# A decoder layer on one core: the prompt's value products one step later, and values stored by block

## The chip, the cores and the metric

The kernel runs on one NeuronCore of a Trainium2 chip. A core has five engines, each with its own queue of instructions that it works through in order: TensorE (PE in the profile; its weight loads are listed apart as PEld), VectorE (DVE), ScalarE (ACT), GpSimd (POOL) and SyncE (SP), which here issues nearly all DMAs. They meet through semaphores. Data are computed on in SBUF (128 partitions); TensorE writes its results to PSUM, eight banks of 2 KB a partition.

The metric is the device time of one execution in microseconds. The kernel before took 1530.84 us in the median of three executions (1525.71 to 1532.65).

## The reference

One layer of a hybrid decoder, for a prompt of 1024 positions and for 8 samples of 8 new positions each, all in fp32. What matters here is the prompt's attention: 16 heads of 64, four query heads to a key/value head, a window of 128 positions, and one learned sink per head that joins the softmax without a value.

```python
def attn_prompt(q, k, v, sinks):
    ...
    kk = jnp.concatenate([jnp.pad(kb, pad)[:, :-1], kb], axis=2)
    vv = jnp.concatenate([jnp.pad(vb, pad)[:, :-1], vb], axis=2)
    diff = jnp.arange(BLOCK)[:, None] + BLOCK - jnp.arange(2 * BLOCK)[None, :]
    band = (diff >= 0) & (diff < WINDOW)
    ...
    o = sink_attention(qb, kk, vv, mask[:, None, None], sinks)

def layer(...):
    h = rmsnorm(x, norm_mix)
    q, k, v, gu, gv, ga, gb = split_in(h @ w_in)
    ...
    s = spatial_gating(jax.nn.gelu(gu), vn, ws, bs)
    merged = jax.nn.sigmoid(ga) * (o @ w_pa) + jax.nn.sigmoid(gb) * (s @ w_pb)
    x = x + merged @ w_out
    f, nconv = conv_ffn(rmsnorm(x, norm_ffn), w_up, conv_w, conv_b, w_down, conv_prev)
    return x + f, nk, nv, nconv, vn
```

A block of 128 queries sees its own block of keys up to the diagonal and the block before it beyond the diagonal. Together these are exactly 128 keys for every query, so one 128 x 128 tile of probabilities holds both: position j of it is the key of the own block where j is at most the query's place, and the key of the block before otherwise.

## The kernel before, in words

Nearly every fp32 number is held as a high and a low part (`split`, lines 39 to 41: ACT casts to the high part, DVE subtracts to get the low one), and a product is made of three matmuls. The 1088 positions go in two groups: the samples with prompt blocks 0 to 3 (group 0), and blocks 4 to 7 (group 1). The program runs through the input projection (to about 440 us), the samples' attention and the attention of group 0 with the gMLP branch's projection between its parts, the attention of group 1 with group 0's merge between its parts (to about 690 us), the output projection and the feed-forward part (to the end).

**Values.** In the projection `v_out` gets 128 positions by 256 values (four key/value heads of 64) for each block, splits them, and stores the tile `ws` of 128 x 4 x 128 (high and low part of each head, 2 KB a partition) in `vd` (line 552). It does the same with differences against the block before (`dvd`). In the attention `values(kv)` loads what a key/value head needs: `vst` with 4 or 5 blocks of values in one DMA (line 950), `dvst` with 3 or 4 blocks of differences in four DMAs of 64 partitions (line 953). Both have two places.

**The loop over steps.** `attention` runs through 16 steps a group, four key/value heads (kv) by four blocks (i). A step has three parts.

- `sc_p` makes the scores (tile `sc`, line 1205, 8 matmuls; 2 KB x 2 of PSUM, one place), copies them to `s` (ACT, line 1213), replaces keys beyond the diagonal by those of the block before (DVE, predicated copy, line 1215; a first block is masked by POOL, line 1218), takes the maximum with the sink (`nm`, line 1221), exponentiates four heads (ACT, line 1224), and scales by the reciprocal of the sums (`dn`, lines 1226 and 1227). `s` has three places.
- `tr_p` transposes the probabilities (`pt`, line 1234, 4 matmuls, one PSUM bank), splits them into `ph` and `pl`, and makes a selection `c` of both on POOL (line 1245, four instructions): the probabilities that belong to the block before.
- `pv_p` makes the value products (`po`, one PSUM bank): four matmuls of `ph` and `pl` with the values (line 1262), then two of `c` with the differences (line 1265), which correct the places of the block before. First blocks have two matmuls (line 1257). ACT copies half of the result (`ot`, line 1268), DVE adds the halves (`of`, line 1273), and a split gives `oh` and `ol`, the attention's output.

Between these parts `fill` puts pieces of other work: in group 0 the branch's projection, in group 1 the merge (matmuls `mm` of line 235, a product `stg` on DVE, loads and stores on SP, weights cast to `wh` and `wl`). A counter deals them out evenly over a number of slots (`slots["of"]`).

The code's order is not quite the order on the engines. The tile layer puts instructions into the queues by its own priorities and costs, so a product may stand a few matmuls ahead of or behind its place in the code. Two places of a tile (`bufs=2`) let a new one be written while the old one is read.

Of the kernel before, what the change touches and what calls it, by code (L numbers as in the profile page):

```python
# [6 lines left out]
F32 = mybir.dt.float32  # L7
F32R = mybir.dt.float32r
# [7 lines left out]
P = 128  # L16
# [6 lines left out]
NKV = 4  # L23
# [11 lines left out]
def layer(tc, a):  # L35
    nc = tc.nc
# [10 lines left out]
    with ExitStack() as top:  # L47
# [280 lines left out]
        dr = lambda name, shape, dt=F32: dram.tile(shape, dt, name=name)  # L328
# [3 lines left out]
        kd = [dr(f"kd{c}", [P, 2, T]) for c in range(2)]  # L332
        gud = [dr(f"gud{c}", [P, T]) for c in range(NG)]
        sgd = [[dr(f"sg{e}d{c}", [P, T]) for c in range(KD)] for e in range(2)]
        vd = dr("vd", [P, NKV, 8, P])
        v3d = dr("v3d", [P, 256])
        dvd = dr("dvd", [P, NKV, 8, P])
        gvd = {name: dr(f"gvd{name}", [P, GW]) for gr in groups for name, _ in gr["toks"]}
        vnd = [dr(f"vnd{gr['g']}", [P, NG, len(gr["toks"]), P]) for gr in groups]
        sd_ = [[dr(f"sd{g}{c}", [P, 2, n]) for c in range(NG)] for g, n in ((0, 576), (1, 512))]  # L340
# [11 lines left out]
        with ExitStack() as ph1:  # L352
# [175 lines left out]
            def v_out(g, i, ps):  # L528
                name = groups[g]["toks"][i][0]
                v = gvp.tile([P, 256], F32, name="gv")  # L530
                S.activation(v, ps, AF.Copy, scale=1.0 if g else rstg[g][:, i:i + 1])
                if name == "s":
                    nc.sync.dma_start(vsd, v[0:NS])
                    for b in range(8):
                        nc.sync.dma_start(a["vsn"][b], v[8 * b:8 * b + 8])
                else:
                    if name == 4:
                        late["v"] = gvp.tile([P, 256], F32, name="gv")
                        nc.sync.dma_start(late["v"], v3d)
                    for to, x in ((vd, v), (dvd, None)):  # L540
                        if x is None and name == 0:
                            continue
                        t = W.sm.tile([P, 4, P], F32, name="ws", bufs=2)
                        tr, four = t.bitcast(F32R), lambda y: y.rearrange("p (h d) -> p h d", d=64)
                        if x is None:
                            x = t[:, :, 64:128]
                            for r, (y, z) in ((0, (v, late["v"])), (64, (late["v"], v))):
                                V.tensor_sub(x[r:r + 64], four(y)[r:r + 64], four(z)[r:r + 64])
                        else:
                            x = four(x)  # L550
                        split(tr[:, :, 0:64], tr[:, :, 64:128], x)
                        nc.sync.dma_start(to[:, :, name], t)
                    late["v"] = v
                    if name == 3:
                        nc.sync.dma_start(v3d, v)
                if name == 7:
                    nc.sync.dma_start(a["vp"], v)
# [362 lines left out]
            def prepare(gr):  # L920

                g, n = gr["g"], gr["n"]
# [3 lines left out]
                at, nk = ((NS, 512), (448, 640))[g]  # L926
# [16 lines left out]
                def values(kv):  # L943

                    def go():
                        if kv < NKV:
                            v = kvp.tile([P, nv, P], F32R, name="vst", bufs=2)
                            d = kvp.tile([P, 2, nd, P], F32R, name="dvst", bufs=2)
                            gr["vst"][kv], gr["dvst"][kv] = v, d
                            nc.sync.dma_start(v.bitcast(F32), vd[:, kv, b0:b0 + nv])  # L950
                            for e in (0, 64):
                                for o in (0, 64):
                                    nc.sync.dma_start(d[o:o + 64, e // 64].bitcast(F32),
                                                      dvd[e:e + 64, kv, b0 + 1:b0 + 1 + nd])
                    return go

                gr["operands"], gr["values"], gr["b0"] = operands, values, b0
# [124 lines left out]
            def attention(gr, pieces):  # L1082
# [3 lines left out]
                if has_s:  # L1086
                    qs, kn, vs, sp = (smp[x] for x in ("qs", "kn", "vs", "p"))
                nblk = 4
                slots = {"n": len(pieces), "done": 0, "at": 0, "of": 40 + (8 if has_s else 0)}

                def fill():
                    slots["at"] += 1
# [96 lines left out]
                with tc.tile_pool(name=f"at{g}", bufs=1) as ap:  # L1189
# [3 lines left out]
                    def sc_p(kv, i):  # L1193
# [12 lines left out]
                                          start=e == 0, stop=e == 1)  # L1206
                        if i == 0:
                            gr["operands"](kv + 1)()
                        if i == 2:
                            gr["values"](kv + 1)()  # L1210
                        s = ap.tile([P, 4, P + 1], F32, name="s", bufs=3)
                        G.tensor_copy(s[:, :, P], late["sinkb"][:, 4 * kv:4 * kv + 4])
# [17 lines left out]
                    def tr_p(kv, i):  # L1230
                        s = st.pop((kv, i))
                        pt = pst.tile([P, 512], F32, name="pt")
                        for h in range(4):
                            PE.transpose(pt[:, h * P:h * P + P], s[:, h, 0:P], ident)
                        ph = ap.tile([P, 512], F32R, name="ph")
                        pl = ap.tile([P, 512], F32R, name="pl")
                        split(ph, pl, pt)
                        parts = []
                        if gr["blk0"] + i:
                            c = ap.tile([P, 512], F32R, name="c")  # L1240
                            cs, fs, ls = (x.rearrange("p (h e q) -> p h e q", h=4, e=2) for x in (c, ph, pl))
                            for src, swap in ((fs, 0), (ls, 1)):
                                for e in range(2):
# [30 lines left out]
                        c0 = soff + P * i  # L1274
                        split(oh[kv][:, :, c0:c0 + P], ol[kv][:, :, c0:c0 + P], of)

                    for i in range(len(steps) + 2):
                        if i >= 2:
                            tr_p(*steps[i - 2])
                        fill()  # L1280
                        if i < len(steps):
                            sc_p(*steps[i])
                        fill()
                        if i >= 2:
                            pv_p(*steps[i - 2])
                if g == 0:
                    mo[1].close()
                    sso.close()
# [650 lines left out]
```

## Time and profile before

| what | us |
|---|---|
| median of three executions | 1530.84 |
| profiled execution, its own time | 1529.31 |
| its span, first to last instruction | 1527.6 |
| samples' attention ahead of the first prompt scores | 465.0 to 494.4 |
| prompt loop of group 0 | 494.4 to 588.0 |
| fillers between the loops | 588.0 to 599.0 |
| prompt loop of group 1 to its last scores | 599.0 to 669.4 |
| its tail, to the last value products | 669.4 to 687.0 |

The profile lists an engine as busy while an instruction of it runs. Matmuls overlap each other (one starts about 0.12 us behind the one before and is listed for about 0.28 us), so PE can look busy in a stretch where it started nothing. Weight loads do not overlap each other like that: where matmuls follow each other without a wait, a weight load is under way all of the time, and idle time of PEld is time lost. A row of waits names the waiting engine, tile and line, then what ended the wait, then the sum in us, how often, and the longest.

### The profile page before, as it was taken

To read this page: it belongs to the slowest core of one execution; us is meant where nothing else is said; L and a number is where in the kernel's file an instruction comes from. 1 tells how busy PE (TensorE), PEld (TensorE's weight loads), DVE (VectorE), ACT (ScalarE), POOL (GpSimd) and SP (SyncE) were. 2 spreads that over 40 slices of the span, in tenths; PEclk is the share of its full clock that TensorE was granted. 3 is DMA by queue.
4 is the path that set the end of the run, shared out by engine and by line. 5 is a ranking of instruction groups with operands and counts; after the bars stand their busy time and mean duration, and the time that the engine had idled before them with its cause. 6 is when DMAs were issued, how large, how long until landed. Compare 5 with 4: busy or idle time off the path is not lost.

```text
span 1527.6 us, 31403 instructions
## 1 busy us (share of the span) xinstructions
PE 1507.0 (99%) x12202; PEld 1489.1 (97%) x12202; DVE 1156.2 (76%) x1918; ACT 823.2 (54%) x1745; POOL 274.9 (18%) x429
## 2 busy tenths in 40 slices
PE   9999999999999999999999999999999999999998
PEld 9999999999998999989999999999999999999997
DVE  6886778756544886889658888898899888785685
ACT  6555764454543674774433555555555556453562
POOL 0000002200120232440122212232232222000002
PEclk9999999999999999999999999999999999999998
DMA  8553447747649857658988432332243226973453
GB/s 285 156 170 126 166 168 257 247 140 270 222 152 327 258 187 217 202 181 301 327 275 275 146 120 92 120 137 100 87 151 107 79 93 214 363 258 96 127 177 130
DMA packets 136357, 286.64 MB, mean 188 GB/s; under 512 B 15248, under 2 KB 43344, under 8 KB 136208
## 3 DMA queue, kind: packets, MB, share of 16 engines
q1 hardware_dynamic: 132176, 281.08, 55.2%
q10 hardware_dynamic: 4032, 3.55, 0.7%
q8 instruction: 96, 1.57, 0.4%
q14 instruction: 53, 0.43, 0.1%
HBM read 195.69 MB, written 90.85 MB: 188 GB/s over the span
## 4 chain that ended last, share of the span: by engine, by line
PE 68%; DVE 5%; ACT 4%; issue 3%; POOL 2%; DMA 2%; SPq 0%; POOLq 0%; ACTq 0%; DVEq 0%
PE st L294 40%; PE dn L1700 13%; PE mm L235 12%; ACT s L1224 2%; POOL c L1245 1%; POOL x L1765 1%; PE sc L1205 1%; PE mx L832 1%; DVE pl L41 1%; DVE nm L1221 1%; DVE s L1227 0%; ACT ot L1268 0%; DVE wl L41 0%; DVE of L1273 0%; DMA wraw<-wpb 0%
## 5 line engine op out<-in xcount | busy, mean ns | idle before, releaser
L294 PE MATMUL st<-th,wh 128*128 128x256 f32 (+1 forms) x2128 | 611.3, 287 | 4.2 <-ACT k L275 2.3
L294 PE MATMUL st<-tl,wh 128*128 128x256 f32 (+1 forms) x2128 | 609.4, 286 | 0.0
L294 PE MATMUL st<-th,wl 128*128 128x256 f32 (+1 forms) x2128 | 608.8, 286 | 0.0
L294 PEld LDWEIGHTS st<-th,wh 128*128 128x128 f32 x2128 | 400.7, 188 | 6.0 <-ACT k L275 3.4
L294 PEld LDWEIGHTS st<-th,wl 128*128 128x128 f32 x2128 | 401.0, 188 | 0.0
L294 PEld LDWEIGHTS st<-tl,wh 128*128 128x128 f32 x2128 | 400.5, 188 | 0.0
L40 ACT CAST wh<-wraw 128x512 fp32r<-128x512 f32 (+2 forms) x204 | 139.6, 694 | 107.0 <-PE st L294 35.4
L41 DVE TENSOR_TENSOR wl<-wraw,wh 128x512 fp32r<-128x512 f32 (+2 forms) x204 | 159.4, 794 | 37.7 <-ACT wh L40 35.5
L1700 PE MATMUL dn<-th,wh 128*128 128x288 f32 (+1 forms) x616 | 176.7, 287 | 0.0
L1700 PE MATMUL dn<-tl,wh 128*128 128x288 f32 (+1 forms) x616 | 176.2, 286 | 0.0
L1700 PE MATMUL dn<-th,wl 128*128 128x288 f32 (+1 forms) x616 | 175.1, 284 | 0.0
L40 ACT CAST wh<-ws 128x512 fp32r<-128x512 f32 x160 | 98.1, 622 | 96.8 <-PE st L294 62.0
L41 DVE TENSOR_TENSOR wl<-ws,wh 128x512 fp32r<-128x512 f32 x160 | 109.5, 697 | 48.5 <-ACT wh L40 46.8
L1700 PEld LDWEIGHTS dn<-th,wl 128*128 128x128 f32 x616 | 115.9, 188 | 0.0
L1700 PEld LDWEIGHTS dn<-tl,wh 128*128 128x128 f32 x616 | 115.7, 188 | 0.0
L1700 PEld LDWEIGHTS dn<-th,wh 128*128 128x128 f32 x616 | 115.6, 188 | 0.0
L282 POOL TENSOR_TENSOR z<-kn,k 128x256 f32<-128x256 f32 (+1 forms) x32 | 29.9, 938 | 320.0 <-ACT kn L277 304.4
L40 ACT CAST th<-traw 128x544 fp32r<-128x544 f32 (+1 forms) x85 | 53.8, 642 | 45.1 <-PE dn L1700 32.6
L41 DVE TENSOR_TENSOR tl<-traw,th 128x544 fp32r<-128x544 f32 (+1 forms) x85 | 61.6, 732 | 21.0 <-ACT th L40 20.6
L235 PE MATMUL mm<-s,wh 128*128 128x256 f32 (+1 forms) x384 | 75.4, 292 | 0.9 <-DMA s<-sd 0.9
L525 PE MATMUL st<-w2h,th 128*128 128x256 f32 x308 | 74.4, 283 | 0.4 <-ACT w2h L40 0.4
L235 PE MATMUL mm<-oh,wh 128*128 128x256 f32 (+1 forms) x256 | 74.0, 289 | 0.0
(292 smaller groups left out, 3178.2 us busy)
## 6 DMA issues: line engine op xcount, KB each, us to landing
wraw<-wt SPq DMA_DIRECT2D x133, 512.0 KB
traw<-td SPq DMA_DIRECT2D x77, 272.0 KB
td<-za SPq DMA_DIRECT2D x22, 544.0 KB
wraw<-wt SPq DMA_DIRECT2D x35, 256.0 KB
upd<-hl SPq DMA_DIRECT2D x14, 512.0 KB
td<-t SPq DMA_DIRECT2D x11, 544.0 KB
qd<-q SPq DMA_DIRECT2D x8, 576.0 KB
q<-qd SPq DMA_DIRECT2D x8, 576.0 KB
```

The lines of the kernel that those rows point to most:

```text
L40: S.copy(hi, src)
L41: V.tensor_sub(lo, src, hi.bitcast(F32))
L235: PE.matmul(ps[:, lo:lo + c1 - c0], u[:, k, :], v[:, c0:c1], start=(k == 0 and i == 0), stop=(k == nk - 1 and i == 2))
L282: op(to, pick(x, to, lo, hi), pick(y, to, lo, hi))
L294: PE.matmul(ps, u[:, kk, :], v, start=first and kk + i == 0, stop=kk == 3 and i == 2, skip_group_check=True)
L525: PE.matmul(ps, u, v[:, k, :], start=k + i == 0, stop=k == KD - 1 and i == 2)
L832: PE.matmul(ps[:, P * i:P * i + P], vn[:, i], late["wst"][:, c, :], start=True, stop=True)
L1205: PE.matmul(ps[:, h, o0:256], q, kst[kv][:, e, k0:cur + P], start=e == 0, stop=e == 1)
L1221: V.tensor_reduce(nm, s, AX.X, ALU.max, negate=True)
L1224: S.activation(s[:, h], s[:, h], AF.Exp, bias=nm[:, h:h + 1], accum_out=dn[:, h:h + 1])
L1245: G.affine_select(cs[w:w + 64, :, e], src[r:r + 64, :, e].bitcast(F32), [[0, 4], [1 - 2 * e, 64]], ALU.is_ge, 0.0, base=-e, channel_multip ...
L1700: PE.matmul(place(m, e), u[:, m, :], v[:, lo:hi], start=new and i + k == 0 and (e == 0 or m % 2 == 0), stop=i == NU - 1 and k == 2, skip_g ...
```

## The change

- The loop makes the value products of a step one iteration later (`pv_p(*steps[i - 3])`), and so has one iteration more at its end, with one filler slot instead of two. The slots are counted as 41 instead of 40 (49 instead of 48 with the samples).
- `ph`, `pl` and `c` get two places each, 6 KB more a partition.
- The values of the next key/value head are loaded in step 3 instead of step 2.
- `vd` and `dvd` lie by block: a block's tile is stored as 128 rows of 2 KB, where each row was four pieces of 512 B, and the loads gather pieces of 512 B, where a partition's row was one piece of 1.5 to 2.5 KB.

```diff
-        vd = dr("vd", [P, NKV, 8, P])
+        vd = dr("vd", [8, P, NKV, P])
...
-        dvd = dr("dvd", [P, NKV, 8, P])
+        dvd = dr("dvd", [8, P, NKV, P])
...
-                        nc.sync.dma_start(to[:, :, name], t)
+                        nc.sync.dma_start(to[name], t)
...
-                            nc.sync.dma_start(v.bitcast(F32), vd[:, kv, b0:b0 + nv])
+                            nc.sync.dma_start(v.bitcast(F32), vd[b0:b0 + nv, :, kv].rearrange("b p d -> p b d"))
...
-                                                      dvd[e:e + 64, kv, b0 + 1:b0 + 1 + nd])
+                                                      dvd[b0 + 1:b0 + 1 + nd, e:e + 64, kv].rearrange(
+                                                          "b p d -> p b d"))
...
-                slots = {"n": len(pieces), "done": 0, "at": 0, "of": 40 + (8 if has_s else 0)}
+                slots = {"n": len(pieces), "done": 0, "at": 0, "of": 41 + (8 if has_s else 0)}
...
-                        if i == 2:
+                        if i == 3:
                             gr["values"](kv + 1)()
...
-                        ph = ap.tile([P, 512], F32R, name="ph")
-                        pl = ap.tile([P, 512], F32R, name="pl")
+                        ph = ap.tile([P, 512], F32R, name="ph", bufs=2)
+                        pl = ap.tile([P, 512], F32R, name="pl", bufs=2)
...
-                            c = ap.tile([P, 512], F32R, name="c")
+                            c = ap.tile([P, 512], F32R, name="c", bufs=2)
...
-                    for i in range(len(steps) + 2):
-                        if i >= 2:
+                    for i in range(len(steps) + 3):
+                        if 2 <= i < len(steps) + 2:
                             tr_p(*steps[i - 2])
                         fill()
                         if i < len(steps):
                             sc_p(*steps[i])
-                        fill()
-                        if i >= 2:
-                            pv_p(*steps[i - 2])
+                        if i < len(steps) + 2:
+                            fill()
+                        if i >= 3:
+                            pv_p(*steps[i - 3])
```

In the rows below the names are the program's tiles as above, a number at a row's start counts the engine's rows, and line numbers of the changed kernel are one higher. First TensorE in the loop of group 1, from a step's transposes to the next value products, before:

```order
4429 L1234 MATMUL pt<-c_ident,s 128x128 x3
4430 L235 MATMUL mm<-oh_6430,wh 128x320
4431 L235 MATMUL mm<-ol_6431,wh 128x320
4432 L235 MATMUL mm<-oh_6430,wl 128x320
4433 L235 MATMUL mm<-oh_6495,wh 128x320
4434 L235 MATMUL mm<-ol_6496,wh 128x320
4435 L1205 MATMUL sc<-kst,q 128x256 x8
4436 L235 MATMUL mm<-oh_6495,wl 128x320
4437 L235 MATMUL mm<-oh_6495,wh 128x320
4438 L235 MATMUL mm<-ol_6496,wh 128x320
4439 L1262 MATMUL po<-ph,vst 128x4x64
```

Here the products read the `ph` made of the transposes at the top. The same stretch in the changed kernel:

```order
4401 L1235 MATMUL pt<-c_ident,s 128x128 x4
4402 L235 MATMUL mm<-ol_6431,wh 128x320
4403 L235 MATMUL mm<-oh_6430,wl 128x320
4404 L235 MATMUL mm<-oh_6430,wh 128x320
4405 L1206 MATMUL sc<-kst,q 128x256 x8
4406 L235 MATMUL mm<-ol_6431,wh 128x320
4407 L235 MATMUL mm<-oh_6430,wl 128x320
4408 L235 MATMUL mm<-oh_6484,wh 128x320
4409 L1263 MATMUL po<-ph,vst 128x4x64
4410 L1263 MATMUL po<-pl,vst 128x4x64
```

The row looks alike, but the products now read the `ph` and `pl` of the transposes one step further up, and all six follow each other where fillers stood between the first two. On VectorE, the last steps of the same loop, before:

```order
745 L1215 COPY_PREDICATED s<-c_mprev,sc 128x4x128
746 L1227 TENSOR_TENSOR s<-s,dn 128x4x128
747 L1273 TENSOR_TENSOR of<-po,ot 64x256 x2
748 L41 TENSOR_TENSOR pl<-pt,ph 128x512
749 L1221 TENSOR_REDUCE nm<-s 128x4
750 L41 TENSOR_TENSOR ol_8564<-of,oh_8563 128x2x128
```

And in the changed kernel:

```order
733 L1216 COPY_PREDICATED s<-c_mprev,sc 128x4x128
734 L1274 TENSOR_TENSOR of<-po,ot 64x256
735 L1222 TENSOR_REDUCE nm<-s 128x4
736 L1274 TENSOR_TENSOR of<-po,ot 64x256
737 L41 TENSOR_TENSOR pl<-pt,ph 128x512
738 L1227 RECIPROCAL dn<-dn 128x4
739 L1228 TENSOR_TENSOR s<-s,dn 128x4x128
740 L41 TENSOR_TENSOR ol_8550<-of,oh_8549 128x2x128
```

A step's maximum moved up to its predicated copy, with only half of an `of` between, and its scaling follows its own maximum instead of the next step's predicated copy.

## The prediction

> **What bounds the kernel now.** I read the page first, then busy time by stage, then the waits of the weight loads in the two prompt loops, then the chain each step of a loop has to pass.
>
> ```profile
> span 1527.6 us, 31403 instructions
> PE 1507.0 (99%) x12202; PEld 1489.1 (97%) x12202; DVE 1156.2 (76%) x1918; ACT 823.2 (54%) x1745; POOL 274.9 (18%) x429
> PE 68%; DVE 5%; ACT 4%; issue 3%; POOL 2%; DMA 2%; SPq 0%; POOLq 0%; ACTq 0%; DVEq 0%
> ```
>
> TensorE is the bound almost everywhere, so only time in which it stands can be won. Busy PE hides that: the chain gives PE 68%, the busy row 99%. Weight loads (PEld) show it better. By stage (columns: PE, PEld, DVE, ACT and POOL busy, clock, DMA share, GB/s):
>
> ```profile
> 512.00:530.00 18.00, 17.91 (x146) 17.57 (x146) 16.03 (x32) 14.31 (x46) 5.86 (x13) 1.00 0.71 225
> 617.00:634.00 17.00, 17.00 (x133) 16.34 (x132) 16.40 (x32) 14.48 (x48) 6.43 (x16) 1.00 0.60 192
> 494.40:588.00 93.60, 91.35 (x717) 86.19 (x716) 76.90 (x147) 63.48 (x200) 28.62 (x71) 1.00 0.63 207
> 588.00:599.00 11.00, 11.00 (x85) 11.00 (x85) 4.35 (x6) 2.01 (x3) 1.25 (x2) 1.00 0.87 273
> 599.00:669.40 70.40, 69.21 (x512) 64.98 (x512) 61.62 (x115) 53.51 (x169) 26.68 (x63) 1.00 0.70 218
> 669.40:687.00 17.60, 16.22 (x120) 14.82 (x119) 13.36 (x26) 10.57 (x30) 8.18 (x15) 1.00 0.51 155
> ```
>
> Between the loops (588 to 599) PEld is busy all of the time, 0.129 us a matmul. In the first loop (494.4 to 588) it is busy 92.1%, in the second (599 to 669.4) 92.3%, in the second's tail, behind its last scores, 84%. The first two rows are the best stretches of each loop: 97.6% and 96.1%. What the weight loads wait for in the first loop, the second, and the second's tail alone:
>
> ```profile
> PEld po L1265 <- POOL c L1245: 2.4, 9, 0.4
> PEld po L1262 <- DVE pl L41: 1.3, 3, 0.5
> ...
> PEld po L1262 <- issue: 0.5, 2, 0.4
> ```
> ```profile
> PEld po L1265 <- POOL c L1245: 5.2, 16, 1.1
> PEld po L1262 <- ACT ph L40: 0.8, 2, 0.5
> ...
> PEld po L1262 <- issue: 0.6, 2, 0.3
> ```
> ```profile
> PEld po L1265 <- POOL c L1245: 2.5, 6, 1.1
> PEld po L1262 <- issue: 0.3, 1, 0.3
> ```
>
> So the value products (po) wait 4.2 us in the first loop and 6.6 in the second, 2.8 of these in the tail. A wait costs more than its idle time:
>
> ```profile
> L1262 PE MATMUL po<-ph,vst x56: 277/283/387, 511.1 to 684.8; 128*128 128x256 f32 x56
> L1265 PE MATMUL po<-c,dvst x56: 277/384/392, 511.6 to 685.7; 128*128 128x256 f32 x56
> ```
>
> The correction products (L1265) take 384 ns in the median, 277 at best. At least 28 of 56 take the longer form: 28 x 0.107 = 3.0 us (an estimate), which I put at 1.2 in the first loop, 1.2 in the second, 0.6 in its tail.
>
> **Products a step later.** Transposes, cast, subtraction and four POOL selects now have a whole step before their products, and ph, pl, c get second places. No instruction is added. All of these po waits can go: 4.2 + 1.2 = 5.4 us in the first loop, 3.8 + 1.2 = 5.0 in the second, 2.8 + 0.6 = 3.4 in its tail, 13.8 in all. What is late next? Prices on PE (chain view of the first loop), DVE and ACT (groups of 600 to 690: busy, mean | idle before):
>
> ```profile
> 507.57 0.44 PE pt L1234 x4
> ...
> 509.03 0.95 PE sc L1205 x8
> ...
> 511.30 0.47 PE po L1262 x4
> ```
> ```profile
> L1273 DVE TENSOR_TENSOR of<-po,ot 64x256 f32<-64x256 f32 x32 | 13.3, 416 | 6.3 <-ACT ot L1268 6.1
> L1227 DVE TENSOR_TENSOR s<-s,dn 128x512 f32<-128x512 f32 x16 | 12.0, 749 | 0.1
> L1215 DVE COPY_PREDICATED s<-c_mprev,sc 128x512 f32<-128x512 int32 x16 | 11.8, 738 | 0.5 <-ACT s L1213 0.4
> L41 DVE TENSOR_TENSOR pl<-pt,ph 128x512 fp32r<-128x512 f32 x16 | 11.0, 689 | 0.4
> L1221 DVE TENSOR_REDUCE nm<-s 128x4 f32<-128x516 f32 x16 | 10.9, 681 | 0.2
> L41 DVE TENSOR_TENSOR wl<-wraw,wh 128x1024 fp32r<-128x1024 f32 x7 | 8.8, 1255 | 0.0
> L41 DVE TENSOR_TENSOR ol<-of,oh 128x256 fp32r<-128x256 f32 x16 | 7.3, 457 | 0.7 <-ACT oh L40 0.5
> L1075 DVE TENSOR_TENSOR stg<-stg,mm 128x576 f32<-128x576 f32 x7 | 5.2, 746 | 5.4 <-PE mm L235 5.4
> L1226 DVE RECIPROCAL dn<-dn 128x4 f32<-128x4 f32 x16 | 2.8, 172 | 2.8 <-ACT s L1224 2.8
> ```
> ```profile
> L1224 ACT ACTIVATE s<-s,nm 128x129 f32<-128x129 f32 x64 | 25.0, 395 | 2.8 <-DVE nm L1221 2.7
> ...
> L40 ACT CAST ph<-pt 128x512 fp32r<-128x512 f32 x16 | 9.4, 587 | 0.3
> ...
> L1213 ACT COPY s<-sc 128x512 f32<-128x512 f32 x16 | 9.3, 582 | 9.2 <-PE sc L1205 9.1
> ```
>
> By the new order a step of the second loop is on PE: scores, 3 fillers, six products (6 x 0.118 = 0.7), about 12 fillers, four transposes, 4 fillers. From the end of scores i to the transposes of i that is 34 fillers x 0.129 = 4.4, two products 1.4, transposes 0.44 and scores 0.95: 7.2 us. Softmax i has to fit: copy 0.58, predicated copy 0.74, half of "of" 0.42, maximum 0.68. On ACT the cast ph of i-1 stands before the exponentials, as in most steps before; it can start when its transposes are done, 0.39 + 0.7 + 1.55 + 0.44 = 3.1 us after the scores. So the exponentials (25.0 / 16 = 1.56) run from 3.7 to 5.2, and reciprocal and scaling end at 6.1: 1.1 us in hand. DVE fits "of", pl and a filler's product (0.75) in the gap; with a weight's subtraction (1.26) as well, scaling ends at 7.3, 0.1 late, and a backlog is carried on. DVE is the nearest limit here: 61.62 of 70.40 us, and in its best stretch 16.40 of 17 (96.5%), which puts the floor at 61.62 / 0.965 = 63.9 us.
>
> So for the second loop I bound the gain by 2.8 (64.98 / 0.961 = 67.6, the share of its best stretch) and 5.0 (all gone), and take 3.5, nearer the lower end since DVE has nearly no room. In the first loop the best share gives 86.19 / 0.976 = 88.3, a gain of 5.3; all gone is 5.4; I take 4.5, because eight weight subtractions fall there too.
>
> **The extra step at the end.** In the second loop the tail now reads scores 15, products 12, 24 fillers, transposes 14, 8 fillers, products 13, transposes 15, products 14, 12 fillers, products 15. PE reaches transposes 15 after 0.39 + 0.7 + 3.1 + 0.44 + 1.03 + 0.7 = 6.4 us; exponentials 15 start behind ph 14 at 5.2 and scaling ends at 7.7: 1.3 of waiting. Products 14 need the one place of po free: "of" 13 stands behind scaling and an "ol" and ends at 9.0, PE is there at 8.2: 0.8. With refills 0.4 that is 2.5 back, of the 3.4 removed: 0.9 stays; bounds 3.4 and -1 (another wait like it). The first loop's tail has 18 to 27 fillers between; I cost it at nothing.
>
> **Fillers and loads.** 41 and 49 slots for 40 and 48 keep the share of fillers per slot; in the samples' stage, ahead of 494.4, one piece of 9 fillers fewer stands: 0 to 1.2 us, I take 0.5. Values move to step 3, still four steps ahead of their first products, since the products moved too. SP, which waits for the last products of the head two before, keeps that wait:
>
> ```profile
> SPq L950 <- PE po L1265: 7.8, 3, 5.0
> ```
> ```profile
> L552 SPq DMA_DIRECT2D vd<-ws x8: 513/516/617, 45.9 to 87.5; - x8
> L950 SPq DMA_DIRECT2D vst<-vd x8: 319/345/631, 475.5 to 646.5; - x8
> ```
>
> Behind it in SP's order stand a filler's store and load and the next weights, as now. An issue of 512 pieces takes 0.51 us, of 128 pieces 0.32. The 15 stores become 128 rows of 2 KB and save 0.2 each, in a stage where nothing of PE waits for them; the 8 value loads and 32 difference loads become pieces of 512 B and cost at most 0.2 more each, 1 us a group of five, with the filler loads, stores and next keys queued behind on SP. Cover is the four steps (some 20 us); I cost it at 0, bounds 0 and 1 us if one such group makes a filler late. If it were gone, PE would wait at the first products of a head.
>
> **Sum.** -3.5 - 4.5 - 0.9 + 0.5 = -8.4 us. The profiled execution took 1529.31 us (span 1527.6 and 1.7 around): 1520.9. The median shown is 1530.84, 1.5 above it, so on that scale 1522.4.
>
> **A rule against it.** Scaling and selects vary:
>
> ```profile
> L1227 DVE TENSOR_TENSOR s<-s,dn x32: 673/692/896, 503.4 to 676.0; 128x512 f32<-128x512 f32 x32
> ```
> ```profile
> L1245 POOL TENSOR_SCALAR_AFFINE_SELECT c<-ph x56: 408/413/877, 508.9 to 684.1; 64x256 fp32r<-64x256 f32 x56
> ```
>
> Scaling is stretched by 0.22 us at worst, a select by 0.47. The Trainium skill (SBUF — State Buffer, Who interferes with whom) says that a VectorE instruction with two SBUF inputs and a GpSimd instruction that reads SBUF share a port pair, and the second to come blocks until the first is done. By that rule a tighter loop makes selects and scaling meet oftener. The median 692 beside 673 shows that DVE has hardly paid so far.
>
> **Rivals.**
> - *DVE takes the place.* If scaling loses a select's 0.41 us in every step, that is 16 x 0.41 = 6.6 us more DVE work in a loop that has 8.8 us of DVE idle now (70.4 - 61.6): the second loop gains nothing, the first half of its 4.5. -2.3 - 0.9 + 0.5 = -2.7: 1528. For it: DVE at 96.5% in the best stretch. Against: 6.1 us of DVE idle in front of "of" comes from late products and goes. By the page's rule the sum would be this one.
> - *All of the waits go.* 13.8 less: 1517. For it: 1.1 us in hand per step. Against: the tail worked out above.
> - *The wait only changes its name.* PE meets transposes, not products, late in each step; nothing is won: 1531. Against: in both loops together the transposes waited for scaling twice, and 7.6 of the 10.8 us in front of products are for POOL, whose work gets a whole step.
>
> ```profile
> PE pt L1234 <- DVE s L1227: 0.5, 2, 0.3
> ```
>
> - *Slower: the softmax chain sets the step.* A step cannot be shorter than the chain less the 2.6 us (3 fillers, products, 12 fillers) behind the next scores. Today a step is 183.6 / 32 = 5.74 us, so this decides from a chain of 8.3 us, 2.2 over the 6.1 worked out, if DVE's backlog grows from step to step, since ACT and DVE work through the steps in a fixed order. At 8.8 us a step is 6.2: +15 us, 1545. For it: steps with both fillers' work reach 7.3 already.
>
> **How the numbers follow.** Chances: forecast 0.50, all gone 0.12, DVE 0.22, name changed 0.06, slower 0.10. Predicted is the forecast, 1522.4. Its own bounds, from -13.8 to about -3, give 1517 to 1528; with the DVE and renamed cases and some 2 us of scatter 1515 to 1531.5; outside lie the slower case and a little of "all gone". A change of 0.5% (7.7 us, under 1523.2) is about what a measurement of this kernel can tell from none. Faster: all gone and six tenths of the forecast, 0.42. Within: the rest of it, DVE and the renamed, 0.48. Slower: 0.10.
>
> **What would show it.** Right: PEld waits of po on POOL, DVE and ACT near 0 in both loops; correction products with a median near 280 ns; the first loop near 89 us, the second (to its last scores) near 67; DVE at 92% or more there. Wrong: transposes (L1235) waiting for scaling, or products for "of"; scaling above 750 ns; value loads late at the first products of a head; a tail longer than now.

## The result, and the profile after

The changed kernel took 1525.6 us in the median of nine executions (1522.6 to 1529.35), beside 1530.84 for the kernel before, also of nine: a ratio of 0.9975, 95% interval [0.9963, 0.9987]. That is 5.2 us by the medians and 3.7 us by the two profiled executions (1529.31 and 1525.6); the forecast was 8.4. So it is faster, by less than the half per cent named as "same", and the time lies in the range. First the page of the changed kernel: span, busy time, and the chain's shares.

```profile
span 1523.9 us, 31423 instructions
PE 1498.7 (98%) x12202; PEld 1485.8 (97%) x12202; DVE 1157.9 (76%) x1918; ACT 821.6 (54%) x1745; POOL 272.3 (18%) x429
PE 62%; DVE 8%; ACT 4%; DMA 4%; issue 3%; POOL 1%; SPq 0%; POOLq 0%; DVEq 0%; ACTq 0%
```

In the chain POOL falls from 2% to 1% and DVE rises from 5% to 8%. These are shares of the whole span, of which 1% is 15 us, so they give a direction and no size. By stage, the columns as before (first loop, fillers between, second loop to its last scores, its tail):

```profile
494.00:588.20 94.20, 88.77 (x726) 86.26 (x726) 77.06 (x147) 64.39 (x200) 30.03 (x70) 1.00 0.65 210
588.20:599.20 11.00, 11.00 (x86) 11.00 (x85) 4.37 (x6) 1.91 (x3) 1.28 (x2) 1.00 0.84 260
599.20:672.00 72.80, 71.59 (x557) 69.61 (x556) 63.33 (x118) 54.87 (x171) 26.96 (x67) 1.00 0.75 223
672.00:686.50 14.50, 12.11 (x85) 11.09 (x84) 10.92 (x22) 8.32 (x28) 4.42 (x11) 0.88 0.54 198
```

PEld is busy 91.6% of the first loop, where it was 92.1%. In the second loop it is busy 95.6%, where it was 92.3%, and 45 matmuls more stand in it. The tail is at 76%, where it was 84%, and its clock is 0.88. What the weight loads wait for, in the first loop, the second, and the tail:

```profile
PEld po L1263 <- ACT ph L40: 1.4, 1, 1.4
PEld pt L1235 <- DVE pl L41: 1.4, 1, 1.4
PEld po L1263 <- ACT s L1214: 1.3, 1, 1.3
PEld pt L1235 <- issue: 1.2, 3, 0.6
PEld pt L1235 <- ACT s L1214: 1.2, 2, 0.7
...
```
```profile
PEld sc L1206 <- DMA q<-qd: 1.1, 1, 1.1
PEld pt L1235 <- issue: 0.9, 3, 0.3
PEld sc L1206 <- DVE s L1216: 0.4, 2, 0.3
...
```
```profile
PEld pt L1235 <- ACT ot L1269: 1.4, 1, 1.4
PEld po L1263 <- issue: 0.7, 1, 0.7
PEld po L1263 <- ACT s L1225: 0.6, 1, 0.6
...
```

The waits for POOL's c are gone everywhere. In the second loop next to nothing replaces them; in the first loop and in the tail others do, in front of the transposes (pt) and of the first product (po). The correction products, the scaling and the selects, by line:

```profile
L1266 PE MATMUL po<-c,dvst x56: 274/280/285, 515.4 to 686.0; 128*128 128x256 f32 x56
L1228 DVE TENSOR_TENSOR s<-s,dn x32: 677/692/890, 503.8 to 679.4; 128x512 f32<-128x512 f32 x32
L1246 POOL TENSOR_SCALAR_AFFINE_SELECT c<-ph x56: 407/412/669, 510.2 to 682.1; 64x256 fp32r<-64x256 f32 x56
```

The correction products fell from 384 to 280 ns in the median; scaling and selects are as they were in the median. Before, 38 of the 56 correction products were long, and the next matmul started 225 ns behind a long one and 117 behind a short one; after, none is long. To compare kernels whose stages begin at different times, I use three stretches between starts of matmuls in the trace: the first from the samples' first scores (464.39 before) to the second loop's first scores (598.82), the second on to the next norm's first matmul into `sc` (790.54), the third to PE's end.

| start to start, us | before | after | difference | forecast |
|---|---|---|---|---|
| span's start to samples' first scores | 464.39 | 465.42 | +1.0 | 0 |
| first stretch: samples' stage, first loop, fillers | 134.43 | 133.63 | -0.8 | -4.0 |
| second stretch: second loop, tail, merge | 191.72 | 188.62 | -3.1 | -4.4 |
| third stretch | 730.49 | 729.69 | -0.8 | 0 |

They add up to -3.7. The first stretch holds 1097 matmuls in both kernels, the second 1461. The forecast fails in the first stretch.

### The profile page after: what moved, and what is told of

It reads as the page before. It is cut to its first block, busy times and chain, and to the rows that moved or that the text cites. A ratio compares the mean times of both kernels' runs of the same rounds, so it can differ in the third digit from the quotient of the medians.

```text
span 1523.9 us, 31423 instructions
## 1 busy us (share of the span) xinstructions
PE 1498.7 (98%) x12202; PEld 1485.8 (97%) x12202; DVE 1157.9 (76%) x1918; ACT 821.6 (54%) x1745; POOL 272.3 (18%) x429
## 4 chain that ended last, share of the span: by engine, by line
PE 62%; DVE 8%; ACT 4%; DMA 4%; issue 3%; POOL 1%; SPq 0%; POOLq 0%; DVEq 0%; ACTq 0%
PE st L294 40%; PE mm L235 11%; PE dn L1702 10%; ACT s L1225 2%; DMA wraw<-wt 2%; DVE wl L41 2%; DVE s L1228 1%; DVE nm L1222 1%; DVE s L1216 1%; POOL x L1767 1%; PE mx L832 1%; DMA q<-qd 1%; DVE pl L41 1%; DVE ol L41 1%; ACT wh L40 1%
## 5 line engine op out<-in xcount | busy, mean ns | idle before, releaser
L235 PE MATMUL mm<-ol,wh 128*128 128x256 f32 (+1 forms) x256 | 74.3, 291 | 0.1
```

Source lines behind the costliest of these rows:

```text
L235: PE.matmul(ps[:, lo:lo + c1 - c0], u[:, k, :], v[:, c0:c1], start=(k == 0 and i == 0), stop=(k == nk - 1 and i == 2))
```

## The experiments

The kernels below were measured in four groups (layout, later products and the two kernels of one group; second places to `ol` on POOL; `ol` on the kernel before and the moved exponentials; the rest, with `ol` on POOL once more), each beside the kernel before, whose median was 1531.0, 1530.68, 1529.09 and 1528.58 us. So medians are compared within a group, and ratios are to the kernel before of the group. My theory once the result was known: the gain comes from the later products in the second loop alone; in the first loop the waits went over to the single places of pt and po. Rivals: the layout gives or costs part of it; the second places alone do it; the first loop did gain and something beside it took the gain.

**The layout alone.** The kernel before with

```diff
-        vd = dr("vd", [P, NKV, 8, P])
+        vd = dr("vd", [8, P, NKV, P])
```

and the same for `dvd`, their stores and loads.

> The kernel before with the values by block alone, products where they were. Theory (the gain lies in the later products, the layout is hidden): the time of the kernel before, within 1.5 us, about 1530.8; second loop with the same 5 us of po waiting for POOL's selects. Rival (the layout carries part of the gain, by its shorter stores): 1526 to 1528. Rival (the layout costs and hides part of the gain, by its loads in short pieces): 1532 to 1533.

Measured: 1531.6 us, ratio 1.0007 [0.9993, 1.0021]; stretches 135.12 and 191.76. Nothing, as the theory said.

**The later products with the old layout.** The changed kernel without those lines.

> The changed kernel with the values in their old layout. Theory: as the changed kernel, about 1525.6. Rival (layout carries part of the gain): 1528 to 1531. Rival (layout costs): 1523 to 1524.

Measured: 1524.41 us, 0.996 [0.9945, 0.9974]; stretches 133.92 and 188.36. All of the gain is here. In the changed kernel an issue of a store takes 342 ns and one of a value load 382 ns in the median, where they took 516 and 345. It shows nowhere in the time.

**The later products in one group only.** With `lag = 3 if g == 1 else 2` (then `g == 0`) in place of the constant 3, in the loop's length, the slots, the values' step and the number of places.

> Later products and second places in group 1's loop only; group 0's loop as before. Theory (the first loop gave nothing, its waits went over to the transposes and to the one place of po): as the changed kernel, 1525 to 1527, second loop and its tail as there. Rival (the first loop did gain, and the samples' stage or the fillers between the loops took it): 1528 to 1530, with po waiting 4 us in the first loop and that loop longer than the changed kernel's.

> Later products and second places in group 0's loop only. Theory: as before, 1530 to 1532, first loop within 0.7 us of before with its waits on pt and on of in place of POOL's selects. Rival (first loop gains): 1527 to 1529.

Measured: group 1 only 1527.07 us, 0.9975 [0.9959, 0.9991], stretches 136.11 and 189.30. Group 0 only 1530.49 us, 1.0006 [0.9991, 1.0021], stretches 134.24 and 190.87. So the later products in the first loop alone gain nothing that the times show, and most of the gain comes from the second. A small gain in the first is not excluded: with both loops changed the same group has 1524.41, 2.7 less than with group 1 only, though the intervals overlap. The first stretch with the old order (before, layout alone, group 1 only) was 134.43, 135.12 and 136.11, and 137.22 with second places alone (next); with the new one, in this section and below, 133.5 to 134.2. By their means that is 1.4 us, 1.9 with the fourth, not 4.

**Second places alone.** The kernel before with `bufs=2` for ph, pl and c.

> The kernel before with second places for ph, pl and c, products where they were, old layout. Theory (products wait because POOL's selects of the same step end late, not because a place is missing): 1530 to 1532, po waiting for POOL's c about 10 us in both loops and the tail as before. Rival (the second places are what counts, since cast, subtraction and selects of the next step may start earlier): 1527 to 1529.

Measured: 1530.01 us, 0.9991 [0.9975, 1.0007]; first stretch 137.22, second 190.62. Places without the later products do nothing that the times show.

**More fillers in the tail.** The edit was a second `fill()` in two iterations.

> The changed kernel with one filler slot more in each of the iterations 16 and 17 of group 1's loop (two slots' work, about 16 matmuls of 0.12 us, moved from behind the tail into it). Theory (the tail's transposes 15 and products 14 wait for lack of fillers, and the window of half clock follows these waits): waits of pt and po in the tail under 0.7 us in place of 2.2, no half clock there, the stretch from the second loop's first scores to the norm's first matmul 186.5 to 187.5 in place of 188.6; 1523 to 1524.5. Rival (the waits only move behind the last products, where these fillers stood; the half clock comes anyway): 1525 to 1526.5.

The tile layer put every instruction on every engine in the same order as in the changed kernel, so the question was not tried. What ran is the changed kernel a second time: 1523.87 us, 0.9948 [0.9933, 0.9963]; stretches 133.69 and 188.62, as in the first profile to 0.1 us.

**The mask of first blocks on DVE.**

```diff
-                            G.affine_select(s[:, :, 0:P], s[:, :, 0:P], [[0, 4], [-1, P]], ALU.is_ge, NEG,
-                                            base=0, channel_multiplier=1)
+                            V.copy_predicated(s[:, :, 0:P], late["mprev"].to_broadcast([P, 4, P]),
+                                              late["neg"][:, 0:1, None].to_broadcast([P, 4, P]))
```

It came from the order in the changed kernel ahead of the longest wait of a transpose on PE. The rows show start, duration, then the idle time before it and what ended it, on POOL, DVE and PE:

```profile
558.84 1.78 POOL L1246 TENSOR_SCALAR_AFFINE_SELECT c<-pl 64x256 fp32r<-64x256 f32 x2
560.69 0.64 POOL L1219 TENSOR_SCALAR_AFFINE_SELECT s<-s 128x512 f32<-128x512 f32 x1
```
```profile
561.36 0.69 DVE L1222 TENSOR_REDUCE nm<-s 128x4 f32<-128x516 f32 x1 [1.49 <-POOL s L1219]
561.96 0.84 DVE L1274 TENSOR_TENSOR of<-po,ot 64x256 f32<-64x256 f32 x2
563.77 0.18 DVE L1227 RECIPROCAL dn<-dn 128x4 f32<-128x4 f32 x1 [0.97 <-ACT s L1225]
563.99 0.69 DVE L1228 TENSOR_TENSOR s<-s,dn 128x512 f32<-128x512 f32 x1
564.60 0.42 DVE L41 TENSOR_TENSOR ol<-of,oh 128x256 fp32r<-128x256 f32 x1
564.93 0.68 DVE L41 TENSOR_TENSOR pl<-pt,ph 128x512 fp32r<-128x512 f32 x1
```
```profile
565.67 0.33 PE L1235 MATMUL pt<-c_ident,s 128*128 128x128 f32 x1 [1.16 <-DVE pl L41]
```

The transposes of the next step need the one place of pt, which is free when pl has read it. On DVE pl stands behind `ol` and the scaling, these behind the reciprocal, which waits for the exponentials, which waited for the maximum of a first block, and that waited for the mask, which stands on POOL behind two selects of c.

> The changed kernel with the mask of a first block as a predicated copy of a constant on DVE (as later blocks have it) in place of POOL's select of 1.9 us. It touches four steps of the first loop. Theory (the first loop's new waits start there: POOL's select delays maximum and exponentials, DVE stands in order behind them, and pl and of, on which the one place of pt and of po depends, come late): the waits of pt for pl and of po for of, 1.2 us each at 541, 565 and 570, shrink to under 0.5; 2 to 3 us less in the first loop, 1522.5 to 1524. Rival (DVE's load as such makes them late): four more DVE instructions of 0.74 us, no gain, 1525 to 1527.

Measured: 1525.7 us, 0.9958 [0.9942, 0.9973]. From the first prompt scores to the second loop's first scores 104.27 us, where the changed kernel had 105.11: 0.8 less, not 2 to 3. (Its samples' stage ran 6.8 us at a clock of 0.5, so its whole first stretch, 137.58, can't be compared.) In the same group the changed kernel's second run took 1523.87, so by itself the mask is no remedy. The mask as an instruction was not slow either: POOL takes 0.63 to 0.70 us for it, not the 1.9 that I expected, and DVE 0.80. What it loses on POOL is its place behind the selects.

**`ol` on POOL**, which takes 16 subtractions a loop off DVE:

```diff
-                        split(oh[kv][:, :, c0:c0 + P], ol[kv][:, :, c0:c0 + P], of)
+                        S.copy(oh[kv][:, :, c0:c0 + P], of)
+                        G.tensor_sub(ol[kv][:, :, c0:c0 + P], of, oh[kv][:, :, c0:c0 + P].bitcast(F32))
```

> The changed kernel with the subtraction that makes ol on POOL in place of DVE (32 instructions of 0.46 us off DVE, 7.3 us in each loop). Rival to the masked blocks (DVE's load as such makes pl and of late): the first loop's waits of pt and po fall by half, 2 to 3 us less, 1522 to 1524. Theory (the masked blocks): they stay within 1 us, 1524.5 to 1526; worse, up to 1529, if the selects of c stand behind ol on POOL for long enough to make products wait again.

> The version with ol on POOL once more, beside the others of this call. If its gain is real: 1519 to 1522, again 3 us or more below the changed kernel; first stretch 132 to 133, second (to the norm's first statistics) 186 to 187.5. If the matmuls' pace in the profiled run made it: 1524 to 1526.

Measured: 1520.33 us, 0.9931 [0.9913, 0.9949], and again 1522.21 us, 0.9957 [0.9939, 0.9974]; stretches 132.65 and 186.29, again 132.92 and 186.62. The changed kernel's second run, in the group of the first, took 1523.87, 3.5 us more; the order that is `ol` deferred (below), in the group of the second, 1.6 more. The intervals overlap. The stretches can't be read singly here: with `ol` on POOL eight matmuls, about 1 us, stand in the second stretch that stood in the first (1089 and 1469). The two together have 318.9 and 319.5 us. Like is compared with like where neither the half clock nor the matmuls' pace (both treated below) differ: 318.9 beside 320.5 with `ol` deferred, 319.5 beside 322.3 with the later products in the old layout. So it wins 1.5 to 2.7 us, and the changed kernel's own profile (322.3) loses 1.6 more by the half clock. DVE's load counts. PE's waits in the first loop only fell from 5.4 to 4.8 us, not by half, so the masked blocks are not ruled out there; as the whole theory they fall.

**The same on the kernel before.**

> The kernel before with the subtraction that makes ol on POOL in place of DVE. Theory (before, the products waited for POOL's selects, and DVE only became the limit once the products had moved): no gain here, since ol stands among the selects on POOL: 1530 to 1535, po still waiting for c 8 us or more in both loops. Rival (DVE was a limit all along, and relieving it is worth 4 us or more by itself, whatever the products do): 1525 to 1527.

Measured: 1534.31 us, 1.0033 [1.0016, 1.0051], slower. Its products wait longer for POOL than before; the rows are PE's, of the second loop and its tail, first before:

```profile
PE po L1265 <- POOL c L1245: 1.5, 3, 0.8
PE po L1265 <- POOL c L1245: 4.6, 7, 1.0
```

So before the change POOL's selects held up the products, and more work on POOL cost 5 us; after it DVE's load does, and the same edit pays.

**Exponentials behind the products.** `sc_p` cut in two, the exponentials and the scaling written behind `pv_p`, so that ACT has ot and ph ahead of exponentials that would hold them up; alone, with `ol` on POOL, and with the mask too:

```diff
+                        if i < len(steps):
+                            ex_p(*steps[i])
```

> The changed kernel with the exponentials and the scaling written behind the value products, so that on ACT ot (which frees po's place) and ph (which frees pt's) stand ahead of exponentials that wait for their maximum. Theory (in the first loop the single places of po and pt come free late because ot and ph stand behind such exponentials): the two waits of po of 1.2 us at 541 and 570 go, samples' first scores to second loop's first scores 131 to 132.5 us in place of 133.6; 1523 to 1524.5. Rival (DVE's load makes of and pl late, ACT's order is no matter): the waits stay, 1525 to 1527.

> Both: exponentials behind the value products on ACT, and ol on POOL. If ACT's order and DVE's load are two causes, the gains add: first stretch 130 to 131.5 us (132.6 with ol on POOL alone), second about 186.3; 1518 to 1519.5. If they are one cause seen twice: as ol on POOL alone, 1520 to 1521.

> Exponentials behind the value products, ol on POOL, and the first blocks' mask on DVE. With ol off DVE the four predicated copies have room, and POOL's select no longer delays the first blocks' maximum by 1.7 us: 1 to 2 us below the version without the mask, 1516.5 to 1518.5, the waits of po in the first loop under 1.5 us in all. Rival (the mask is not on the path): the same time as that version, within 1 us.

Measured: 1526.02 us, 0.997 [0.9951, 0.9988]; with `ol` 1524.86, 0.9975 [0.9957, 0.9992]; with both 1522.77, 0.9953 [0.9937, 0.9969]. PE's waits in the first loop, the changed kernel ahead and the moved exponentials alone behind it:

```profile
PE pt L1235 <- DVE pl L41: 2.2, 3, 1.2
PE po L1263 <- DVE of L1274: 1.2, 1, 1.2
PE po L1263 <- ACT s L1214: 1.1, 1, 1.1
PE pt L1235 <- DVE s L1228: 0.9, 3, 0.4
```
```profile
PE pt L1239 <- DVE pl L41: 2.6, 3, 1.2
PE pt L1239 <- DVE s L1232: 1.6, 2, 1.2
PE pt L1239 <- ACT ot L1273: 0.7, 1, 0.7
```

The waits of po went, as I expected, and those of pt grew: 5.4 us of waits became 4.9, and no time was won. Beside `ol` on POOL the move even costs: its two stretches, 134.10 and 189.64, are 4.2 us longer than those of the second profile with `ol` alone, at the same pace. The wait changed its name a second time. Within this group the mask, beside both, gave 2.1 us.

**`ol` and `oh` written behind the next transposes.** On DVE it swaps `ol` and `pl` at the three places where transposes wait for pl, on ACT `ph` and `oh` at two; PE's order is the same.

> The changed kernel with the split into oh and ol written behind the next transposes and their split. On DVE this swaps ol and pl at three places of the first loop, the three at which transposes wait for pl; nothing else moves there. If DVE's order is what keeps the one place of pt (theory): these three waits, 2.2 us in all, shrink by 0.4 each, 1.2 us in all, and the first stretch (samples' first scores to second loop's first scores) goes from 133.6 to 132.4 or less; 1524 to 1525. If the waits only change name again (rival: the softmax chain through ACT and DVE sets the first loop's steps, whichever wait shows it): the same sum of waits there, 1525 to 1526.5.

Measured: 1523.84 us, 0.9968 [0.9951, 0.9985]; stretches 133.50 and 186.98. The waits for pl fell from 2.2 to 1.4 us, one of po grew from 1.1 to 1.6, and the first stretch is unchanged. By its median the run fits the theory (1524 to 1525), by the first stretch and the waits the rival, and these are what the edit acts on: order within DVE moves the wait. What the second stretch won is a window of half clock that is not there (below).

**`ol` on POOL and the mask on DVE**, exponentials where they were.

> ol on POOL and the first blocks' mask on DVE, the exponentials where they were. If the mask is worth 2 us once DVE has room (it gave that beside the moved exponentials): 1517.5 to 1519.5, first stretch near 131. If not: 1519 to 1522, as ol on POOL alone.

Measured: 1519.88 us, 0.9937 [0.9914, 0.996], 8.7 us below the kernel before of its group; stretches 130.06 and 186.95. By the median this lies in the range expected for no gain; by the first stretch it is beyond the 131 expected for one. That stretch is 3.6 us shorter than in the changed kernel, of which 1.0 is the eight matmuls that went to the second. To compare the same work, I take the first loop from its first scores to its last value product: before, changed, mask on DVE alone, `ol` on POOL alone, and both:

```profile
494.33:587.41 93.08, 90.83 (x714) 85.67 (x713) 76.59 (x146) 62.99 (x199) 28.37 (x68) 1.00 0.64 209
493.94:587.63 93.69, 88.26 (x722) 85.75 (x721) 76.56 (x147) 63.82 (x199) 29.81 (x68) 1.00 0.65 211
495.58:588.43 92.85, 88.16 (x722) 85.98 (x721) 79.38 (x151) 63.28 (x199) 29.15 (x64) 1.00 0.64 205
490.82:583.74 92.92, 88.05 (x723) 85.76 (x721) 71.77 (x132) 63.83 (x199) 42.74 (x83) 1.00 0.66 215
495.84:586.43 90.59, 87.89 (x722) 85.81 (x721) 74.25 (x136) 63.28 (x199) 40.21 (x79) 1.00 0.67 216
```

Four of the rows have the same 721 weight loads, 86 us of them. Each edit alone shortens the loop by 0.8 us, both by 3.1. (Four more profiles with the new order in this loop have 93.2 to 93.5, so alone each is worth about 0.6.) The medians agree: beside `ol` on POOL the mask is worth 2.3 us (1522.21 to 1519.88), without it nothing. DVE is busy 82% of the loop in the changed kernel and 82% with both edits, so its total alone does not explain the loop; that the time at which its work comes is the rest is my reading, and no run tests it apart. The row of both is one profile, and the intervals of the times overlap. PE's waits there in this kernel are half of those after the change:

```profile
PE po L1263 <- DVE of L1274: 1.0, 2, 0.8
PE pt L1235 <- DVE s L1228: 0.8, 2, 0.5
PE po L1263 <- ACT s L1214: 0.8, 1, 0.8
```

## Why the prediction was right or wrong

- **What bounds the kernel**: right. PE's idle time in front of the value products was the thing to win, and POOL's selects were its cause. The price of a wait beyond its idle time was there too, on 38 correction products, where I had put 28.
- **The first loop, -4.5: wrong, and the step that failed.** With the filler term of +0.5 it stood for -4.0; the pair of profiles shows -0.8, the means of all profiles -1.4 to -1.9, and the run with later products in group 0 only shows no gain. From first scores to last value product the loop went from 93.08 to 93.69 us with eight matmuls more, 1.0 us at 0.129: 0.4 won, not 4.5. The step took the share of PEld in the loop's best 18 us as what the whole loop could reach, and left the first blocks out. In the changed kernel the softmax chain of a first block (mask on POOL behind selects, maximum and scaling on DVE, exponentials on ACT) holds up pl and of, and with them the single places of pt and po. I had excluded "the wait only changes its name" because transposes waited for the scaling only twice before. That was no evidence: a wait that ends before another one does is in no list. For this loop that rival, given 0.06, came closest; the run with `ol` on POOL and the mask on DVE got 3.1 us out of it. How much the masked blocks and DVE's load each carry stays open, since either edit alone gives about 0.6.
- **The second loop, -3.5: right.** Its 45 additional matmuls, at 0.129 us, stand for 5.8 us, so that its 72.8 us correspond to 67.0 with the work of before, 3.4 less than 70.4: the forecast was 67. DVE is busy 63.33 of 72.80 us, 87%, not the 92% that I named.
- **The tail, -0.9: wrong sign.** From the last scores to the last value product it went from 16.47 us with 109 matmuls to 14.08 with 79; the 30 fewer stand for 3.9 us, so it is 1.5 longer. The waits were sized well: transposes 15 waited 1.28 us (forecast 1.3), products 14 0.47 (0.8); products 13 waited 0.42, which I had not counted. Most of the loss is the half clock (below): the later products in the old layout, with the same order and no half clock, have 12.84 us there, 0.2 longer than before instead of 0.9 shorter. Against it, the merge behind the tail, with 15 matmuls fewer (1.9 us), went from 104.87 to 101.70, so that 1.2 were won by its pace (below too): -3.4 + 1.5 - 1.2 = -3.1. That the second stretch of this pair came near the forecast is in part luck, since half clock and pace nearly cancel.
- **Fillers, loads and stores**: the samples' stage and the first loop exchange one piece of 9 fillers, as forecast, and both ends are in the first stretch; its cost was not seen. The layout costs nothing (1.0007 by itself).
- **The rule on the port pair** (the Trainium skill, SBUF — State Buffer, Who interferes with whom): by it scaling should have been stretched oftener. The median is 692 ns before and after, and the longest 890, where it was 896. The traces do agree that the two stretch each other: a scaling during which no instruction of POOL ran took at most 693 ns in the profiles of before, changed and `ol` on POOL, and all longer ones had one beside them, up to 1225 ns with `ol` on POOL. Selects of c ran at most 417 ns without scaling, `ol` or `wl` beside them; longer than 500 were 23 of 112 before, and 14 after. So they were stretched more rarely after the change, not oftener.
- **DVE takes the place** (0.22): not by longer instructions, as I had written it, but as a limit, yes. Taking `ol` off DVE wins 1.5 to 2.7 us after the change, by stretches, and costs 5 before it. **All waits go** and **slower**: no.

## What to carry to other kernels

When a step gives up waiting for one engine, look for the next single place (here one PSUM bank each for pt and po) and write down what stands ahead of the instruction that frees it, on its own queue. A wait that is covered by a longer one is in no list of waits, so its absence there doesn't bound what comes next. Try the relief of the next engine together with the change: an edit that costs 5 us alone won about 2 behind it, and two edits that give 0.6 each in a loop gave 3 together. Before stretches are compared, count that the same work stands in both.

## What the runs showed of the hardware

**A window of half clock after short waits.** In the changed kernel the clock falls to 0.50 for 3.41 us from 682.2 on; the run with `ol` deferred, whose second loop and tail stand in the same order, has none. The rows (682.2 to 685.6, first the changed kernel, then that run):

```profile
682.20:685.60 3.40, 3.28 (x17) 2.99 (x16) 1.87 (x5) 0.99 (x2) 1.23 (x3) 0.50 0.33 125
```
```profile
682.20:685.60 3.40, 3.31 (x29) 3.12 (x28) 1.99 (x5) 1.51 (x3) 0.00 (x0) 1.00 0.00 0
```

17 matmuls instead of 29. The second stretch is 188.62 us with it and 186.98 without, 1.64 apart, with the merge at the same pace. Six profiles have this tail on PE (changed kernel, its repeat, later products in the old layout, group 1 only, mask, `ol` deferred); four show the window, beginning between 680 and 683, and no profile with another loop's end does, but for the one with moved exponentials, whose tail waits in the same way. Ahead of the window there is no long pause: the longest from one matmul's start to the next is 1.56 us, and about as long in the runs without a window.

What differs is how the short waits lie on a grid. In every profile all changes of the granted clock are whole multiples of 3.413 us apart (in the changed kernel 105.37, 682.22 and 1518.49 us, 169 and 245 steps), so the grid can be laid over the tail. Two of its steps, first in the changed kernel, where the second is followed by the half clock, then with `ol` deferred, where neither is:

```profile
675.40:678.81 3.41, 2.88 (x24) 2.54 (x22) 3.20 (x6) 1.88 (x8) 0.90 (x3) 1.00 0.76 251
678.81:682.22 3.41, 1.66 (x13) 1.28 (x13) 2.50 (x6) 2.14 (x6) 1.24 (x4) 1.00 1.01 381
```
```profile
672.52:675.93 3.41, 1.83 (x14) 1.46 (x12) 2.76 (x7) 3.12 (x11) 1.64 (x4) 1.00 0.99 338
675.93:679.35 3.42, 2.54 (x18) 2.17 (x19) 2.70 (x7) 1.48 (x3) 1.71 (x4) 1.00 0.97 375
```

PEld is busy 38% of the step ahead of the half clock; without it the same waits are split into steps of 43% and 64%. All seventeen profiles agree. Up to 1500 us the clock falls fifteen times in them, each time behind a step with PEld busy for 42% or less; of some 7400 steps at full clock one with 41% and all with 43% or more were not followed by a fall. The six tails have steps of 35, 38, 38 and 42% with a window, 43 and 44% without. So the same order has the window or not by where the grid happens to lie. Where the limit comes from, no run shows. The Trainium skill (TensorE: Matmul & The Clock Gate, HAM oscillation — how this bites in real kernels) gives as the rule no idle gaps of TensorE above about 3.4 us; here, in this tail, the clock fell with none longer than 1.56 us. Its free-running window of 3413 ns (the same page, What's actually happening) agrees with the grid.

**Two paces of the same matmuls at the same clock.** In an uninterrupted row of matmuls of 256 columns one starts 118 ns behind the other in some profiles and 113 in others, at a granted clock of 1.00. The rows are from the merge behind the tail, before and after:

```profile
700.00:710.00 10.00, 10.00 (x87) 10.00 (x86) 10.00 (x16) 4.59 (x7) 0.00 (x0) 1.00 0.79 269
```
```profile
700.00:710.00 10.00, 10.00 (x91) 10.00 (x90) 10.00 (x15) 4.28 (x6) 0.00 (x0) 1.00 0.90 310
```

The pace holds over tens of microseconds. The kernel with the later products in the old layout has the changed kernel's order of matmuls in this merge and the slower pace, and lost 1.3 us there against it. Between 1280 and 1470 us it differs again: five of the seventeen profiles have the slower pace there, and their third stretch is 732.6 to 733.4 us; in the other twelve it is 729.6 to 730.8. That is about 3 us of scatter in kernels whose differences are 1 to 5 us, and it lies in no edit. What sets the pace stays open. With the paces alike and no half clock the second stretch is 190.6 to 190.9 with the old order (group 0 only, second places only) and 186.98 with the new one (`ol` deferred): 3.8 us won. At the slower pace it is 191.7 with the old order (before, layout alone) and 188.36 with the new (later products in the old layout): 3.4. The forecast, tail included, was 4.4.
